# The modulation's matrix-vector products, moved from branches and projections into the attentions

## The chip, the cores and the metric

The kernel runs on one core of a Trainium2 chip. The metric is the device time of one execution in microseconds (us); given is the median of three runs. The engines are TensorE (PE, with its weight loads PEld), VectorE (DVE), ScalarE (ACT), GpSimd (POOL) and SyncE (SP), which here issues the DMAs. Each engine works through its own queue in order.

## The reference, cut to what matters

A first block of two layers with 512 tokens `x` and 256 tokens of context `ctx`, 2048 wide, then a second block. Everything is float32.

```python
for l in range(DEPTH):                                   # two layers
    sh_l, sc_l, g_l = split(silu(c)     @ w_mod[l] + b_mod[l], 3)
    sh_c, sc_c, g_c = split(silu(c_ctx) @ w_mod[l] + b_mod[l], 3)
    hl = xl * (1 + sc_l) + sh_l;  hc = xc * (1 + sc_c) + sh_c
    parts_l = split(hl @ w_in[l]);  parts_c = ...        # conv, attention, pooling
    att = differential attention of 8 heads over context and tokens
    out = concat(conv branch, attention, pooling branch) @ w_out[l]
    xl = layernorm(alpha * xl + g_l * out_l)             # the same for the context in layer 0
return second_block(xl, c)                               # modulated by one more product, w_ada
```

The modulations are products of a vector of 2048 with a matrix of 2048 x 6144: 48 columns of 128 values for each vector and layer. For `c` and `c_ctx` in layer 0 they are called `l0` and `c0`, in layer 1 `l1` and `c1`, and for the second block `s`. Columns 0 to 31 give shift and scale, 32 to 47 the gate. In layer 1 the gate of the context isn't needed.

## The kernel before

**Products on PE.** A float32 product is made of three matmuls: each 512 columns of weights are loaded (L158), rounded to the part `whi` on ACT (L159), and the rest `wlo` is subtracted on POOL or DVE (L139). A *unit* is 128 output columns for all tokens: 16 steps over the depth by three matmuls, for tokens (512 columns) and context (256), so 48 pairs at L166. Its sums stand in two of four `ps_m` buffers.

**Stages.** The first 322 us make layer 0's scale and shift and begin its first units. Then come: layer 0's attention (322 to 1070 us), its convolution and pooling tiles (`branch`, to 1336), the output projection of tokens (`w_out_group`, to about 1497) and context (to 1645), layer 1's attention (to 2345), its branches (to 2548), its projection, the second block. `conv_tile` makes a unit and copies it to `uu` on ACT (L514), makes a second one and multiplies it with `uu` on DVE into `V` (L521), then makes a third (L528).

**Dots.** Columns of the modulation that are not needed at once are made by `dots` (L776 to L812). It goes over four quarters of the depth. At a quarter's start it loads the conditioning vectors (`gv`, L787) and activates them (ACT L789, DVE L790). Then each step loads one 128 x 512 piece of weights into `gw` (L798) and makes one dot for each vector: on DVE in one instruction (L806), or, for every `pool_every`-th dot, as a product on POOL (L802) and a sum on ACT (L803). All these write one scratch buffer, tag `gj`. `gw` has `bufs` buffers, 2 in the attentions and 4 elsewhere.

**What sets the order.** `along(steps, n)` names the steps that go along with the units, `n` per unit; `advance` emits them with a priority lowered by 800, `finish` emits what is left. A scheduler then sets the order of each engine by priority and by when operands and buffers come free in its own model of time; on the chip the order is fixed. The widest products in layer 1's branches go another way (`gemv`): 1 MB of weights, 2048 wide, one DVE instruction each (L292), 30 of them.

Of the kernel before, what the change touches and what calls it, by code (L numbers as in the profile page):

```python
# [18 lines left out]
DRAM = bass.MemoryType.DRAM  # L19
# [26 lines left out]
def mixer_stack_kernel(ctx: ExitStack, tc: tile.TileContext, a: dict, out: bass.AP):  # L46
# [10 lines left out]

# [1 line left out]
    def ps_m(w=512):  # L59
# [10 lines left out]

# [1 line left out]
    ident = const.tile([128, 128], F32, name="ident")  # L72
# [54 lines left out]

# [1 line left out]
    Yd = [dp.tile([128, NT], F32, name=f"yd{k}") for k in range(KT)]  # L129
# [6 lines left out]

# [1 line left out]
    def sub_lo(lo, src, hi, eng):  # L138
# [9 lines left out]
    def load_chunk(*srcs, narrow=None):  # L148
        """512 columns at a time: the load, the part that float32r keeps and the exact rest"""
        n = 1 if narrow else 2  # L150
        hi, lo = (
            narrow.tile([128, 512], F32R, name=f"n{x}", tag=f"n{x}", bufs=2) if narrow else
            wp.tile([128, 1024], F32R, name=f"w{x}", tag=f"w{x}", bufs=3) for x in ("hi", "lo")
        )
        for i in range(n):
            sl = slice(i * 512, (i + 1) * 512)
            raw = wp.tile([128, 512], F32, name="wraw", tag="wraw", bufs=4)
            nc.sync.dma_start(raw, srcs[i] if len(srcs) == n else srcs[0][:, sl])  # L158
            nc.scalar.copy(hi[:, sl], raw)  # L159
            sub_lo(lo[:, sl], raw, hi[:, sl], lo_engine())  # L160
        return hi, lo
# [6 lines left out]
    def operands(*parts, c0=0):  # L168
        """parts: (psum columns, tiles by k) of a product's moving side"""
        return lambda k: [(ps, tuple(t[k][:, i, c0:c0 + ps.shape[-1]] for i in (0, 1))) for ps, t in parts]  # L170

    side = {"steps": iter(()), "n": 0, "late": 800}  # work of other engines that goes along with the units

# [35 lines left out]
    def side_units(n, zero=None):  # L209
        """psum of column tiles that are summed side by side, up to five with the zeros that let two of  # L210
        the narrow sums share a bank"""
        us = [Unit() for _ in range(n)]
        cs = ps_s()
        if zero is None:
            narrow = (cs[:, 0, :NCX], cs[:, 1, :NCX], ps_t()[:, :NCX], ps_v()[:, :NCX])
        else:
            narrow = [cs[:, i // 2, (i % 2) * NCX:(i % 2 + 1) * NCX] for i in range(4)] + [ps_v()[:, :NCX]]
            for b in range(2):
                nc.tensor.matmul(cs[:, b], zero[:, :128], zero, start=True, stop=False)
        for i, u in enumerate(us):  # L220
            u.lat = ps_m() if i < 4 else ps_t()
            u.cx = narrow[i]
            u.shared = zero is not None and i < 4
        us[0].close = cs if zero is not None else None
        return us
# [22 lines left out]
    def silu2(dst, src, tmp):  # L248
        """dst = 2 * silu(src)"""
        nc.scalar.activation(tmp, src, AF.Tanh, scale=0.5)  # L250
        nc.vector.scalar_tensor_tensor(dst, tmp, 1.0, src, op0=ALU.add, op1=ALU.mult)

# [1 line left out]
    mods = {}  # L254
# [8 lines left out]
    def silu_cvec(xp, c):  # L263
        """2 * silu of a conditioning vector that lies on all partitions"""
        t = xp.tile([128, 2, 512], F32, name="cth", tag="gjunk", bufs=1)
        for h in range(4):
            sl = slice(h * 512, (h + 1) * 512)
            nc.scalar.activation(t[:, h % 2], c[:, sl], AF.Tanh, scale=0.5)
            nc.vector.scalar_tensor_tensor(c[:, sl], t[:, h % 2], 1.0, c[:, sl], op0=ALU.add, op1=ALU.mult)

    def cvecs(xp, *idx):
        cs = [load_cvec(xp, i, f"ca{n}") for n, i in enumerate(idx)]
        for c in cs:
            silu_cvec(xp, c)
        return cs

# [8 lines left out]
    def dot(xp, wm, ca, dst, scale=0.5, last=False, split=False):  # L285
        """dst = scale * wm . ca; the last use of wm may overwrite it"""
        if last and split:
# [6 lines left out]
    def gemv(xp, src, vecs, wm_bufs=2, split=False):  # L294
        """vecs: (row vector on all partitions, modulation, bias, column)"""
        wm = load_gemv(xp, src, wm_bufs)
# [5 lines left out]
    def mod_row(name, c0, dst):  # L302
        """16 columns of a modulation tile as one row in DRAM"""
        tp = ps_t()
# [5 lines left out]
    def fold(name, g, b):  # L310
        """from 1+scale and shift to the scale and shift of the normalized rows"""
        m = mods[name]
# [7 lines left out]

# [1 line left out]
    def rope(tp, dst, ps):  # L322
# [174 lines left out]

# [1 line left out]
    def early_gate(xp, g):  # L499
        """a gate of layer 0 that was multiplied before the shifts were known"""  # L500
        t = xp.tile([128, NT], F32, name="pgr", tag="pgr", bufs=1)
# [86 lines left out]

# [1 line left out]
    def y_tiles(pool_, name, n, tag, ks=KT):  # L590
# [10 lines left out]
    def w_out_group(rp, w, Y, toks, res, gate, alpha, bufs=4, raw=False):  # L601
        """toks: (token tile of Y, row id); res(row, cc) -> residual chunk; returns normalized rows"""
        n = len(toks)
# [43 lines left out]
    def make_h(rp, rs, H, G, B, c0=0):  # L647
        """transposes the normalized rows, scales them and splits them into H"""
        n = len(rs)
# [43 lines left out]

    # =======================================================================
    # first block, layer 0
    # =======================================================================
    L, R = "left", "right"
# [11 lines left out]
    with pool("start", R) as sp:  # L709
# [10 lines left out]

        # the products with the scaled rows start before the shifts are known: the pool gates
        # get theirs later, as a bias
        zf = sp.tile([128, 512], F32, name="zf")
# [52 lines left out]
    def dots(xp, vecs, scale, srcs, dst, bufs, pool_every=0):  # L776
        """dst[v][:, i] = scale * srcs[i] . vecs[v], 512 columns at a time; a generator of the steps"""
        n = len(srcs)
# [47 lines left out]
    with pool("attn0", R) as ap_:  # L826
        along(itertools.chain(
            dots(ap_, ("sh_l", "sh_c"), 1.0, [a["w_gateT"][g] for g in range(8)], [pgb[:, 0], pgb[:, 1]], 2, 1),
            mod_dots1(ap_, 0, 32, 48, 2, 1),
        ), 3)  # L830
        attention(ap_, ap_, 0, w0, H, Hc, started=us)
# [27 lines left out]
    with pool("dots1", R) as gp:  # L859
        along(mod_dots1(gp, 1, 0, 20, 4), 10)  # L860
        branch(xp, xp, 0, H, Hc, NT, steps[1:])
        finish()
# [6 lines left out]
    new_mod("s")  # L869
    along(mod_dots1(rp, 1, 20, 32, 4), 2)  # L870
    rs = w_out_group(rp, a["w_out"][0], Y, [(t, t) for t in range(4)], res_dram(rp, a["x"]), "l0", ALPHA_1)
# [10 lines left out]
    Yc = [load_y(rp, t, NL, NCX, k) for k, t in zip(KORDER, y_tiles(cp, "yc0_", NCX, "c"))]  # L882
    along(mod_dots2(rp, 0, 2, 4), 1)
    rs = w_out_group(rp, a["w_out"][0], Yc, [(0, 0), (1, 1)], res_dram(rp, a["ctx"]), "c0", ALPHA_1)
# [7 lines left out]

    # =======================================================================
    # first block, layer 1
    # =======================================================================
    lo_plan["cycle"] = "P"
    with pool("attn1", L) as ap_:
        along(mod_dots2(ap_, 2, 34, 2, 1), 4)
        attention(ap_, aq, 1, a["w_in"][1], H, Hc)
        finish()  # L900
    es_q.close()
    xp = es_h.enter_context(pool("conv1", R))
    branch(xp, xa, 1, H, None, NL, steps[:1])
    with pool("gemv1", L) as gp:
        cl, cs = cvecs(gp, 0, 2)
        todo = [(a["w_mod"][1][n], [(cl, "l1", "b_mod1", n)]) for n in range(32, 48)]
        todo += [(a["w_ada"][0][n], [(cs, "s", "b_ada", n)]) for n in range(34, 48)]
        for i in range(4):
            for src, vecs in todo[8 * i:8 * i + 8]:
                gemv(gp, src, vecs)  # L910
            branch(xp, xa, 1, H, None, NL, steps[i + 1:i + 2])
        mod_row("l1", 32, "l1")
        mod_row("s", 32, "s")
        F_s = fold("s", P("ln_g1"), P("ln_b1"))
    es_y = ExitStack()
# [30 lines left out]

    # =======================================================================
    # second block
    # =======================================================================
    def proj(n):  # L950
# [251 lines left out]
def _layout(v):  # L1202
    """inputs of the program: the arrays of the reference, laid out; and constants of the shapes"""
    f = np.float32
# [91 lines left out]
```

## Time and profile before

| what | us |
|---|---|
| median of 3 runs | 3651.74 (3650.06 to 3652.78) |
| span of the profiled execution | 3643.0 |
| PE busy in it | 3384.8 |
| DVE busy | 2550.5 |
| POOL busy | 2063.3 |
| ACT busy | 1541.6 |
| dots on DVE (L806), 264 | 262.9 |
| dots' products on POOL (L802), 320 | 437.7 |
| their sums on ACT (L803), 320 | 201.9 |

The median lies 8.7 us above the span. Busy times of engines overlap; a wait of PE is what lengthens the span, since PE is busy nearly throughout.

### The profile page before, as it was taken

How to read it: one execution, taken by the hardware profiler on the slowest of the kernel's cores; microseconds unless marked ns; L12 is line 12 of the kernel's file. 1: busy time of each engine (PE TensorE's matmuls, PEld its weight loads, DVE VectorE, ACT ScalarE, POOL GpSimd, SP SyncE). 2: the span in 40 equal slices, each digit the busy share in tenths (PEclk: the TensorE clock that was granted, in tenths of full speed). 3: DMA queues.
4: the chain of work that ended last, by engine and by line, in shares of the span. 5: the costliest groups of instructions: out<-in, count | busy, mean ns of one | idle time of the engine just before them, and what ended most of it. 6: DMA issues, size and time to landing. Idle time of an engine off the chain costs nothing.

```text
span 3643.0 us, 47811 instructions
## 1 busy us (share of the span) xinstructions
PE 3384.8 (93%) x16462; PEld 2740.1 (75%) x16462; DVE 2550.5 (70%) x3817; ACT 1541.6 (42%) x3206; POOL 2063.3 (57%) x1420
## 2 busy tenths in 40 slices
PE   5779999999998788999999999999999899999997
PEld 4668778888887676778777777777778677777765
DVE  9994666666648888775566564485577798985666
ACT  4433666666531122244565553322445323244343
POOL 6665676666624543257777753478776344434432
PEclk8889999999999899999999999999999999999998
DMA  7542333323236556663444422486765222222565
GB/s 258 205 167 80 100 97 95 94 92 97 77 114 194 161 189 222 186 228 125 133 135 132 149 96 68 148 308 239 239 227 195 76 87 81 81 79 99 179 224 186
DMA packets 269140, 541.03 MB, mean 149 GB/s; under 512 B 30080, under 2 KB 37088, under 8 KB 260704
## 3 DMA queue, kind: packets, MB, share of 16 engines
q1 hardware_dynamic: 268896, 537.97, 44.7%
q8 instruction: 129, 2.11, 0.2%
q14 instruction: 115, 0.94, 0.1%
HBM read 508.05 MB, written 29.80 MB: 148 GB/s over the span
## 4 chain that ended last, share of the span: by engine, by line
PE 53%; DVE 24%; DMA 10%; issue 7%; POOL 3%; ACT 2%; SPq 0%; DVEq 0%; POOLq 0%; ACTq 0%
PE ps_m L166 39%; DVE acc L985 5%; DMA wraw<-in_w_out_dram 5%; DVE gpr L806 4%; PE ps_s L395 3%; DVE gjunk L292 2%; PE ps_s L392 2%; PE ps_v L433 2%; DVE wlo L139 2%; DVE h L139 1%; POOL wlo L139 1%; PE ps_t L423 1%; ACT whi L159 1%; DVE hf L766 1%; DVE wm L292 1%
## 5 line engine op out<-in xcount | busy, mean ns | idle before, releaser
L139 POOL TENSOR_TENSOR wlo<-wraw,whi 128x512 fp32r<-128x512 f32 x760 | 1121.4, 1492 | 914.4 <-ACT whi L159 808.4
L166 PE MATMUL ps_m<-h,whi 128*128 128x512 f32 (+1 forms) x4608 | 1577.7, 399 | 2.6 <-DVE qr L325 1.1
L166 PEld LDWEIGHTS ps_m<-h,whi 128*128 128x128 f32 x4608 | 867.9, 191 | 196.7 <-issue 9.9
L159 ACT CAST whi<-wraw 128x512 fp32r<-128x512 f32 x1032 | 602.9, 618 | 838.4 <-DMA wraw<-in_w_out_dram 264.8
L166 PE MATMUL ps_m<-h,wlo 128*128 128x512 f32 (+1 forms) x2304 | 914.9, 398 | 0.0
L802 POOL TENSOR_TENSOR gpr<-gw,gv 128x512 f32<-128x512 f32 x320 | 437.7, 1368 | 261.8 <-ACT gpr L803 207.6
L166 PE MATMUL ps_m<-hc,whi 128*128 128x256 f32 x1920 | 537.3, 286 | 0.0
L166 PEld LDWEIGHTS ps_m<-h,wlo 128*128 128x128 f32 x2304 | 439.4, 191 | 96.2 <-issue 2.7
L139 DVE TENSOR_TENSOR wlo<-wraw,whi 128x512 fp32r<-128x512 f32 x272 | 246.5, 917 | 180.1 <-ACT whi L159 178.7
L166 PEld LDWEIGHTS ps_m<-hc,whi 128*128 128x128 f32 x1920 | 363.1, 191 | 9.7 <-issue 5.8
L803 ACT ACTIVATE gpr<-gpr 128x512 f32<-128x512 f32 x320 | 201.9, 631 | 205.3 <-POOL gpr L802 202.6
L166 PE MATMUL ps_m<-hc,wlo 128*128 128x256 f32 x960 | 275.7, 287 | 0.0
L806 DVE SCALAR_TENSOR_TENSOR gpr<-gw,gv 128x512 f32<-128x512 f32 x264 | 262.9, 996 | 8.2 <-DMA gw<-in_w_ada_dram 1.7
L985 DVE SCALAR_TENSOR_TENSOR acc<-gu,pack,acc 128x511 f32<-128x511 f32 (+24 forms) x240 | 235.4, 993 | 5.4
L624 PE MATMUL ps_m<-wlo,y 128*128 128x512 f32 x512 | 206.9, 405 | 17.6 <-POOL wlo L139 11.1
L401 DVE TENSOR_REDUCE mx<-ps_s 128x1 f32<-128x768 f32 (+1 forms) x160 | 135.0, 844 | 113.4 <-PE ps_s L395 112.8
L625 PE MATMUL ps_m<-whi,y 128*128 128x512 f32 x512 | 202.9, 397 | 2.4 <-DVE y L139 1.6
L166 PEld LDWEIGHTS ps_m<-hc,wlo 128*128 128x128 f32 x960 | 183.7, 191 | 6.2 <-issue 4.3
L406 ACT ACTIVATE E<-ps_s,nb 128x768 f32<-128x768 f32 (+1 forms) x160 | 130.5, 816 | 133.4 <-DVE nb L403 130.4
L623 PE MATMUL ps_m<-whi,y 128*128 128x512 f32 x512 | 182.2, 398 | 0.4 <-ACT whi L159 0.2
L428 DVE TENSOR_TENSOR aTl<-ps_t,aTh 128x384 fp32r<-128x384 f32 (+1 forms) x144 | 77.2, 536 | 145.7 <-ACT aTh L427 145.4
L240 PE MATMUL ps_m<-h,whi 128*128 128x512 f32 x320 | 125.0, 438 | 58.1 <-DVE h L139 29.4
(372 smaller groups left out, 5778.6 us busy)
## 6 DMA issues: line engine op xcount, KB each, us to landing
wraw<-in_w_in_dram SPq DMA_DIRECT2D x640, 256.0 KB, 2.9
wraw<-in_w_out_dram SPq DMA_DIRECT2D x384, 256.0 KB, 3.5
wm<-in_w_mod_dram SPq DMA_DIRECT2D x48, 1024.0 KB, 5.7
gw<-in_w_mod_dram SPq DMA_DIRECT2D x192, 256.0 KB, 3.4
gw<-in_w_ada_dram SPq DMA_DIRECT2D x136, 256.0 KB, 3.1
wm<-in_w_ada_dram SPq DMA_DIRECT2D x14, 1024.0 KB, 5.5
yraw<-yd SPq DMA_DIRECT2D x40, 256.0 KB, 3.4
gw<-in_w_gateT_dram SPq DMA_DIRECT2D x32, 256.0 KB, 3.0
```

The lines of the kernel that those rows point to most:

```text
L139: eng.tensor_tensor(lo, src, hi.bitcast(F32), op=ALU.subtract)
L159: nc.scalar.copy(hi[:, sl], raw)
L166: nc.tensor.matmul(ps, w, mv[part], start=(first and p == 0), stop=(last and p == 2))
L401: nc.vector.reduce_max(mx, sv, axis=AX.XY)
L406: nc.scalar.activation(e[:, :nk].rearrange("p (c n) -> p c n", c=nch), sv, AF.Exp, bias=nb, scale=0.125, accum_out=d,)
L623: nc.tensor.matmul(ps, yh, hi[:, sl], start=(k == 0), stop=False)
L624: nc.tensor.matmul(ps, yh, lo[:, sl], start=False, stop=False)
L625: nc.tensor.matmul(ps, yl, hi[:, sl], start=False, stop=(k == KT - 1))
L802: nc.gpsimd.tensor_tensor(pr, w, t, op=ALU.mult)
L803: nc.scalar.activation(pr, pr, AF.Copy, scale=scale, accum_out=part[v][:, i:i + 1])
L806: nc.vector.scalar_tensor_tensor(junk, w, scale, t, op0=ALU.mult, op1=ALU.mult, accum_out=part[v][:, i:i + 1])
L985: nc.vector.scalar_tensor_tensor(A[:, s:], U[:, :NL - s], wj(i), A[:, s:], op0=ALU.mult, op1=ALU.add)
```

## The change

It moves dots between stages, in the arguments of `along`, and removes the `gemv` loop of layer 1's branches with `cvecs`. Comments go too, so that lines from about 275 on have numbers six lower in the changed file (L806 becomes L800, L802 L796, L803 L797, L798 L792, L514 L508, L521 L515).

```diff
@@ layer 0, attention
             mod_dots1(ap_, 0, 32, 48, 2, 1),
-        ), 3)
+            mod_dots1(ap_, 1, 0, 32, 2, 3),
+        ), 8)
         attention(ap_, ap_, 0, w0, H, Hc, started=us)
@@ layer 0, branches
-        along(mod_dots1(gp, 1, 0, 20, 4), 10)
+        along(mod_dots(gp, ("l1",), (0,), a["w_mod"][1], "b_mod1", 32, 48, 4), 4)
         branch(xp, xp, 0, H, Hc, NT, steps[1:])
@@ layer 0, projection of the tokens, then of the context
-    along(mod_dots1(rp, 1, 20, 32, 4), 2)
+    along(mod_dots2(rp, 0, 4, 4), 1)
...
-    along(mod_dots2(rp, 0, 2, 4), 1)
+    along(mod_dots2(rp, 4, 8, 4), 1)
@@ layer 1, attention
-        along(mod_dots2(ap_, 2, 34, 2, 1), 4)
+        along(itertools.chain(mod_dots2(ap_, 8, 28, 2, 2), mod_dots2(ap_, 28, 48, 2, 2)), 5)
         attention(ap_, aq, 1, a["w_in"][1], H, Hc)
@@ layer 1, branches
-    with pool("gemv1", L) as gp:
-        cl, cs = cvecs(gp, 0, 2)
-        todo = [(a["w_mod"][1][n], [(cl, "l1", "b_mod1", n)]) for n in range(32, 48)]
-        todo += [(a["w_ada"][0][n], [(cs, "s", "b_ada", n)]) for n in range(34, 48)]
-        for i in range(4):
-            for src, vecs in todo[8 * i:8 * i + 8]:
-                gemv(gp, src, vecs)
-            branch(xp, xa, 1, H, None, NL, steps[i + 1:i + 2])
-        mod_row("l1", 32, "l1")
+    branch(xp, xa, 1, H, None, NL, steps[1:5])
+    mod_row("l1", 32, "l1")
```

The dots by stage, before and after:

| stage | on POOL and ACT | on DVE | loads of `gw` |
|---|---|---|---|
| layer 0, attention | 192, then 280 | 0, then 168 | 96, then 224 |
| layer 0, branches | 0 | 160, then 64 | 80, then 64 |
| layer 0, projection, tokens | 0 | 96, then 16 | 48, then 16 |
| layer 0, projection, context | 0 | 8, then 16 | 8, then 16 |
| layer 1, attention | 128, then 80 | 0, then 80 | 128, then 160 |
| layer 1, branches | 0 | 30 wide, then 0 | 30 of 1 MB, then 0 |

The order of the engines at the end of layer 0's attention. First ACT, before: the copies of the first convolution unit to `uu` stand right behind attention's last operations (`rt`, `o2`).

```order
L439 ACTIVATE o2_9349<-ps_v_9341 128x256
L442 CAST o2h_9351<-o2_9349 128x256
L159 CAST whi_10088<-wraw_10090 128x512
L159 CAST whi_10088<-wraw_10094 128x512
L453 COPY rt_9149<-ps_v_9355 128x256
L455 ACTIVATE rt_9149<-rt_9149,eps_t_78 128x256
L514 COPY uu_9951<-ps_m_9833 128x512
L514 COPY uu_9951<-ps_m_9834 128x256
```

ACT, changed: behind the same `rt` stand the sums of the remaining layer-1 dots, some 70 rows of L797, and then the copies.

```order
L447 COPY rt_10152<-ps_v_10358 128x256
L449 ACTIVATE rt_10152<-rt_10152,eps_t_78 128x256
...
L797 ACTIVATE gpr_10005,gpart_9413<-gpr_10005 128x512
L797 ACTIVATE gpr_10016,gpart_9413<-gpr_10016 128x512
L797 ACTIVATE gpr_10025,gpart_9413<-gpr_10025 128x512
L508 COPY uu_10858<-ps_m_10740 128x512
L508 COPY uu_10858<-ps_m_10741 128x256
```

The copies moved behind the sums. On DVE, before: attention's last operation (`SG`), then the branch.

```order
L460 RECIPROCAL rt_9149<-rt_9149 128x256
L461 TENSOR_TENSOR SG_9025<-SG_9025,rt_9149 128x256
L519 MEMSET V_9954 128x1
L520 MEMSET V_9954 128x1
L519 MEMSET V_9954 128x1
L520 MEMSET V_9954 128x1
L504 TENSOR_SCALAR pgr_10206<-pgr_10206,pgb_167 128x512
```

On DVE, changed: 133 dots between the two, the last of them of the fourth quarter (`gpart` holds a quarter's partial sums).

```order
L455 TENSOR_TENSOR SG_10028<-SG_10028,rt_10152 128x256
L800 SCALAR_TENSOR_TENSOR gpr_6745,mod_c1_166<-gw_6741,gv1_6162 128x512
L800 SCALAR_TENSOR_TENSOR gpr_6752,mod_c1_166<-gw_6747,gv1_6162 128x512
...
L800 SCALAR_TENSOR_TENSOR gpr_10023,gpart_9413<-gw_10021,gv0_9403 128x512
L806 TENSOR_TENSOR mod_l1_165<-mod_l1_165,gpart_9413 128x32
...
L513 MEMSET V_10861 128x1
L514 MEMSET V_10861 128x1
```

The branch's first operations moved behind them. POOL's 68 products and the loads of these dots stand in one piece too, with no remainder of weights (`wlo`) and no other load between them. PE's own queue, changed, where the third unit (`ps_m_10993`) follows the second (`ps_m_10863`):

```order
L166 MATMUL ps_m_10862<-h0_15_146,wlo_10923 128x512
L166 MATMUL ps_m_10863<-hc0_15_162,wlo_10923 128x256
L299 MATMUL ps_t_11126<-ident_69,mod_l0_163 16x128
L166 MATMUL ps_m_10993<-h0_0_131,whi_10995 128x512 x2
L166 MATMUL ps_m_10993<-h0_0_131,wlo_10996 128x512
```

The units follow each other on PE as before; nothing moved in between.

## Rows read from the trace of the kernel before

**Rows 1.** The page, busy time, share of the span and instructions of each engine.
```profile
PE 3384.8 (93%) x16462; PEld 2740.1 (75%) x16462; DVE 2550.5 (70%) x3817; ACT 1541.6 (42%) x3206; POOL 2063.3 (57%) x1420
```

**Rows 2.** Stretches: length, busy PE, PEld, DVE, ACT, POOL (instructions), PE clock, DMA, GB/s.
```profile
322.00:1070.00 748.00, 740.22 (x4083) 607.88 (x4082) 459.67 (x756) 439.18 (x1015) 480.27 (x356) 0.99 0.29 91
1083.00:1336.00 253.00, 208.68 (x1090) 178.82 (x1089) 223.03 (x441) 45.18 (x83) 118.44 (x78) 0.90 0.56 176
1336.00:1497.00 161.00, 151.11 (x621) 119.71 (x620) 137.80 (x284) 45.18 (x86) 51.95 (x38) 0.96 0.70 220
...
1645.00:2345.00 700.00, 698.55 (x3527) 557.72 (x3527) 381.44 (x592) 359.26 (x788) 444.52 (x335) 1.00 0.36 115
2345.00:2548.00 203.00, 192.59 (x798) 152.62 (x797) 141.89 (x147) 54.60 (x97) 159.38 (x93) 0.97 0.79 281
```

**Rows 3.** PE's waits, 1083 to 1336: line waited for, us, times, longest.
```profile
PE ps_v L166 <- ACT dh L569: 26.5, 4, 10.7
PE ps_v L166 <- DVE yp L584: 13.1, 4, 5.5
```

**Rows 4.** Timeline of ACT at attention's end: start, us, operation, idle before.
```profile
1070.12 0.84 ACT L514 COPY uu<-ps_m 128x512 f32<-128x512 f32 x2
```

**Rows 5.** Timeline of DVE there.
```profile
1072.04 0.43 DVE L461 TENSOR_TENSOR SG<-SG,rt 128x256 f32<-128x256 f32 x1
...
1084.52 1.01 DVE L521 TENSOR_TENSOR V<-ps_m,uu 128x512 f32<-128x512 f32 x2
```

**Rows 6.** Timeline of PE there.
```profile
1083.32 0.39 PE L166 MATMUL ps_m<-h,whi 128*128 128x512 f32 x1
```

**Rows 7.** Line L802 in layer 0's attention: count, ns min/median/max, first and last start.
```profile
L802 POOL TENSOR_TENSOR gpr<-gw,gv x192: 1271/1292/2039, 346.2 to 981.0; 128x512 f32<-128x512 f32 x192
```

**Rows 8.** Timeline of POOL in head 7.
```profile
949.55 1.30 POOL L802 TENSOR_TENSOR gpr<-gw,gv 128x512 f32<-128x512 f32 x1 [0.83 <-ACT gpr L803]
951.68 1.29 POOL L802 TENSOR_TENSOR gpr<-gw,gv 128x512 f32<-128x512 f32 x1 [0.83 <-ACT gpr L803]
```

**Rows 9.** Line L803 in layer 0's attention.
```profile
L803 ACT ACTIVATE gpr<-gpr x192: 613/632/661, 347.5 to 982.3; 128x512 f32<-128x512 f32 x192
L803 ACT ACTIVATION_READ_ACCUMULATOR gpr<-gpr x192: 183/187/218, 348.1 to 982.9; 128x1 f32 x192
```

**Rows 10.** Timeline of DVE in the layer-0 branches, then of POOL.
```profile
1103.28 1.66 DVE L806 SCALAR_TENSOR_TENSOR gpr<-gw,gv 128x512 f32<-128x512 f32 x1
...
1115.02 0.69 DVE L806 SCALAR_TENSOR_TENSOR gpr<-gw,gv 128x512 f32<-128x512 f32 x1
...
1115.76 0.69 DVE L806 SCALAR_TENSOR_TENSOR gpr<-gw,gv 128x512 f32<-128x512 f32 x1
...
1099.25 5.14 POOL L139 TENSOR_TENSOR wlo<-wraw,whi 128x512 fp32r<-128x512 f32 x3
1117.03 1.11 POOL L565 TENSOR_TENSOR dd<-S,rc 128x512 f32<-128x512 f32 x1 [12.64 <-DMA yd<-yc]
```

**Rows 11.** DMA issues, median us to landing: layer 0's attention, then its branches.
```profile
gw<-in_w_mod_dram SPq DMA_DIRECT2D x64, 256.0 KB, 3.0
...
gw<-in_w_mod_dram SPq DMA_DIRECT2D x79, 256.0 KB, 3.7
```

**Rows 12.** Timeline of all engines where a quarter ends and the next begins.
```profile
766.79 0.19 ACT L803 ACTIVATION_READ_ACCUMULATOR gpr<-gpr 128x1 f32 x1
...
770.81 1.50 POOL L802 TENSOR_TENSOR gpr<-gw,gv 128x512 f32<-128x512 f32 x1 [4.75 <-ACT E L406]
```

**Rows 13.** Stretches of the layer-0 branches, columns as in rows 2.
```profile
1099.85:1335.10 235.25, 190.93 (x988) 163.21 (x987) 206.54 (x414) 39.18 (x73) 108.54 (x71) 0.89 0.55 171
...
1250.00:1260.00 10.00, 3.01 (x9) 2.63 (x10) 8.91 (x13) 1.86 (x3) 9.39 (x8) 0.56 0.41 128
```

**Rows 14.** Groups of DVE, 2345 to 2548: busy us, mean ns, idle before, releasers.
```profile
L292 DVE SCALAR_TENSOR_TENSOR wm<-wm,ca 128x2048 f32<-128x2048 f32 x30 | 78.5, 2615 | 24.5 <-DMA wm<-in_w_ada_dram 13.9 <-DMA wm<-in_w_mod_dram 10.5
```

**Rows 15.** PE's waits in layer 0's projections, 1336 to 1645.
```profile
PE ps_s L624 <- DVE wlo L139: 9.7, 4, 4.7
```

More of the change, by code (lines that the diff above doesn't have):

```diff
@@ L269, in silu_cvec @@
             nc.vector.scalar_tensor_tensor(c[:, sl], t[:, h % 2], 1.0, c[:, sl], op0=ALU.add, op1=ALU.mult)
[L271 to L275, printed above, removed]
     def new_mod(name):
@@ L903, in mixer_stack_kernel @@
     branch(xp, xa, 1, H, None, NL, steps[:1])
-    with pool("gemv1", L) as gp:
-        cl, cs = cvecs(gp, 0, 2)
-        todo = [(a["w_mod"][1][n], [(cl, "l1", "b_mod1", n)]) for n in range(32, 48)]
-        todo += [(a["w_ada"][0][n], [(cs, "s", "b_ada", n)]) for n in range(34, 48)]
-        for i in range(4):
-            for src, vecs in todo[8 * i:8 * i + 8]:
-                gemv(gp, src, vecs)
-            branch(xp, xa, 1, H, None, NL, steps[i + 1:i + 2])
-        mod_row("l1", 32, "l1")
-        mod_row("s", 32, "s")
-        F_s = fold("s", P("ln_g1"), P("ln_b1"))
+    branch(xp, xa, 1, H, None, NL, steps[1:5])
+    mod_row("l1", 32, "l1")
+    mod_row("s", 32, "s")
+    F_s = fold("s", P("ln_g1"), P("ln_b1"))
     es_y = ExitStack()
```

## The prediction, written before the result was known

> **What bounds the kernel now.** The summary of the page comes first: TensorE (PE) is busy 93% of a span of 3643.0 us, VectorE (DVE) 70% [rows 1]. So a gain must come out of the 7% in which PE idles, and a loss comes from whatever makes PE idle more. Next, the stretches [rows 2]. In layer 0's attention PE is busy 740 of 748 us, in layer 1's 698.6 of 700, and there DVE, ScalarE (ACT) and GpSimd (POOL) all have room: 440 to 480 us of 748. In the layer-0 branches (1083 to 1336) PE is busy 209 of 253 us while DVE is busy 223 and the granted clock is 0.90. In the projection behind it and in the layer-1 branches PE misses 10 us each. Third, whom PE waits for in the branches [rows 3]: 40 us in eight waits, on ACT and DVE in the pooling tiles, work that queues behind the dots on DVE. So dots do cost time in the branches, and the attentions have idle engines. That is the case for the change. Last I ask, engine by engine, where the moved dots stand in the new program, since every engine works its queue in order.
>
> **Where they stand.** Layer 0's own dots run on POOL and ACT. They are 192 pairs, from 346.2 to 981.0 us, and attention's last DVE operation starts at 1072.04 [rows 5, 7]. The change asks for eight steps per unit instead of three, but the order of all engines is the same up to the last head: these 192 pairs keep their slots. Layer 1's dots for both vectors (4 quarters of 32 steps, a step being one load and two dots) therefore start only at about 985 us. Most of the first quarter is mixed with head 7; its last five steps and the other three quarters stand behind attention's last operation, in one piece, on DVE, POOL, ACT and the DMA queue alike: 68 POOL dots with their ACT halves and 133 DVE dots. I call it the tail.
>
> **What waits for it.** In the kernel before ACT copies the first convolution unit out of PSUM at 1070.12, right behind attention [rows 4]. PE, which finished the second unit, starts the third at 1083.3 [rows 6], in the two buffers that this copy freed (there are four, two per unit). In the changed kernel the same copy stands behind the last ACT half of the tail, and DVE's first branch operations stand behind its last dot. PE's queue holds nothing else between the second and third unit. So PE stops near 1083 until the tail is done; the tail has no cover.
>
> **Length of the tail.** All dots write one scratch buffer, so they form one chain over the engines.
> - A POOL-ACT dot takes 2.13 us from start to start (949.55 to 951.68: 1.30 on POOL, 0.63 and 0.19 on ACT) [rows 8, 9].
> - A DVE dot takes 0.74 us with POOL quiet (1115.02 to 1115.76) and 1.66 with POOL at work [rows 10]. In the tail the one buffer keeps the two from overlapping, so 0.74 holds.
> - Every third dot goes to POOL, so three steps of two dots cost 2.87, 2.87 and 1.48 us, 2.41 on average.
> - A step's weights come into one of two buffers, and a load can be issued only when the step two before it is done. A load lands in 3.0 us here, 3.7 where DMA is busier [rows 11]; with the handing over I take 3.15. A step ends at the later of (the step before) and (the step two before, plus 3.15), plus its dots. Followed through 32 steps that gives 94.7 us behind the first load, or 2.96 a step: two buffers don't hide the loads.
> - At a quarter's start the conditioning vectors are reloaded and activated: 3.8 us from the last half dot (766.98) to the next dot (770.81) [rows 12]. I take 5, since other work helps less here. A quarter is 100 us.
>
> The end is 1072 + 5 (head 7 delayed by 42 DVE dots of its own) + 5 x 3 + 3 x 100 = 1392 us, so PE starts the third unit at 1393 instead of 1083: **+310**. Bounds: with all loads hidden a quarter is 78 + 4 = 82, the end 1333 and the term +250. With 3.7 for a load and 7.5 at a boundary it is 103.9 - 3.7 + 7.5, say 108, plus 10 more for head 7, and the term is +345.
>
> The Trainium skill, page "DMA: Bandwidth & Descriptors", section "Anatomy of one DMA", fits a load (on POOL's path; here SyncE issues) as 2.0 us plus bytes over 436 GB/s. For 256 KB that is 2.6 us, under the 3.0 of the row. By it the three quarters would be about 17 us shorter; the row decides.
>
> **The other terms.**
> - Clock: in the 10 us in which PE worked 3.0 the granted clock was 0.56 [rows 13], near the lower of the two levels (1.2 of 2.4 GHz). After the stall some matmuls run at half speed: **+4** (0 to +8).
> - Layer-0 branches: DVE loses 96 of 160 dots there, some 100 us at a mean near 1.05. From the end of the third unit 235 us are left for ten units [rows 13]; a unit is 48 pairs of matmuls at 0.348 us, 167 us in all, so 68 are lost. The pooling chains' latency stays, the queue in front of them goes: **-28** (-45 to +5, the latter if loads for 48 fewer steps make no odds and the new order is worse).
> - Projection of layer 0: 96 dots become 16; PE waits there 9.7 us on DVE's remainder of the weights [rows 15] and a few more on others; the context's projection gets 8 dots more: **-10** (-18 to 0).
> - Layer-1 branches: the 30 wide products go (78.5 us of DVE) with 30 loads of 1 MB [rows 14], for 10 us of PE idle: **-10** (-16 to 0).
> - Layer-1 attention: 128 POOL dots become 80, and 80 DVE dots come. Their last stands well ahead of attention's last operation in every queue, so no tail. DVE goes from 381 to at most 381 + 80 x 1.74 = 520 of 700 us: **+3** (0 to +10).
>
> Sum: 310 + 4 - 28 - 10 - 10 + 3 = **+269**. The span becomes 3912; the median lies 8.7 above the profiled span, so 3921 us.
>
> **Rivals.**
> 1. *The tail is shorter* because loads land faster or overlap better with an idle DMA. Its price is +250 for the stall, so 3651.7 + 250 - 41 = 3861. For it: nothing but these loads is queued there. Against: 3.0 is already the median of 64 such loads beside attention [rows 11].
> 2. *The tail is longer*: loads at 3.7, boundaries at 7.5, head 7 late. +345 - 41 gives 3956; if the branches gain nothing either, 3997. For it: 3.7 and more was seen in the branches. Against: DMA was busy 0.56 there [rows 2] and carries one stream here.
> 3. *It pays, as meant*: PE isn't held. It needs the copy of the first unit ahead of the tail, or PE work for 300 us that needs no eviction. Then only the gains stay, -28 - 10 - 10 + 8 = -40, so about 3612. It decides from where the tail's end falls before 1083, which even 68 x 2.13 + 133 x 0.74 = 243 us of bare dots exclude. Only a misread order leaves room.
> 4. *DVE and POOL slow each other in the attentions.* A dot on DVE went from 0.69 to 1.66 us beside POOL [rows 10]. If each of the 42 + 80 DVE dots there cost PE half of that 1 us, it is +60, so about 3980. Against: PE waited for hardly anything in 748 and 700 us. The Trainium skill, "GPSIMD Engine Reference", section "Specifications", says that POOL shares its SBUF interfaces with VectorE and contends with DVE instructions of two SBUF inputs; the dots are such, and the trace agrees.
>
> **How the numbers follow.** Forecast 0.78, rival 1 0.07, rival 2 0.08, rival 4 0.03, rival 3 0.03, no change (gains and losses cancel) 0.01. From the terms' ends the forecast spans about 3870 to 3965. I widen it to 3845 to 4000 for rivals 1, 2 and 4. Within 0.2%, about what a measurement can tell: 0.01; faster 0.03; slower 0.96.
>
> **What would show it.** Right: a stretch from about 1085 to 1390 with PE at zero, DVE with runs of dots some 0.74 or 2.9 us apart, PE's longest wait there naming ACT's copy of the first unit, and a low clock behind it; branches behind it with less wait on the pooling chain; no waits in layer 1's attention. Wrong: PE busy in that stretch, or the first unit's copy near 1075. If the stall is there but its length is off, the loads' landing and the period of three steps (8.9 us with loads, 7.2 without) tell which term failed.

## The result, and the profile after

The changed kernel takes 3926.7 us (3922.3 to 3930.3) against 3652.3 us for the kernel before on the same chip: the ratio is 1.075, with a 95% interval of 1.0736 to 1.0763. The forecast was 3921 us. The profiled span is 3920.5 us instead of 3643.0, so 277.5 us have to be found.

They can be placed by the times at which PE begins a part of its work, since its order is the same up to layer 1: the third unit of the branches (1083.3 before), the token projection (1335.2), the context's (1540.3), its end (1646.9), layer 1's projection (2549.3).

| part | before, us | after, us | difference | forecast |
|---|---|---|---|---|
| to the third unit | 1083.3 | 1376.8 | +293.5 | +310 |
| rest of layer 0's branches, clock in it | 251.9 | 227.3 | -24.6 | +4 - 28 |
| layer 0's projections | 311.7 | 299.7 | -12.0 | -10 |
| layer 1's attention and branches | 902.4 | 924.0 | +21.6 | +3 - 10 |
| the rest | 1093.7 | 1092.7 | -1.0 | 0 |

The stretches of the changed kernel, columns as in [rows 2]:

```profile
1084.00:1376.00 292.00, 1.42 (x9) 0.98 (x7) 99.88 (x278) 56.26 (x148) 90.68 (x72) 0.51 0.34 100
1376.00:1386.00 10.00, 9.21 (x45) 7.95 (x46) 7.33 (x28) 3.82 (x10) 4.13 (x2) 0.82 0.61 180
1376.80:1604.10 227.30, 199.56 (x1081) 173.20 (x1082) 128.37 (x252) 43.64 (x82) 106.09 (x77) 0.92 0.57 178
1604.10:1796.90 192.80, 183.54 (x770) 146.19 (x769) 98.33 (x167) 52.13 (x98) 60.18 (x45) 0.98 0.56 185
1796.90:1903.80 106.90, 99.72 (x449) 79.11 (x448) 76.97 (x98) 46.45 (x79) 61.16 (x44) 0.97 0.66 221
1903.80:2640.00 736.20, 709.29 (x3517) 557.30 (x3516) 441.87 (x760) 328.06 (x694) 383.18 (x285) 1.00 0.39 122
2640.00:2827.80 187.80, 187.39 (x805) 150.15 (x804) 31.63 (x49) 49.96 (x90) 115.07 (x93) 1.00 0.40 129
```

The first of them is the stall: 292 us with 9 matmuls, DVE busy a third of it, POOL not even that, DMA at 0.34, and the granted clock 0.51, near the lower of its two levels (1.2 of 2.4 GHz). The last two are layer 1's attention and its branches. Before, they were:

```profile
1646.90:2345.00 698.10, 696.65 (x3519) 556.17 (x3518) 381.15 (x592) 358.22 (x787) 442.75 (x334) 1.00 0.36 115
2345.00:2549.30 204.30, 193.89 (x803) 153.68 (x802) 141.89 (x147) 54.60 (x97) 159.38 (x93) 0.97 0.79 281
```

For the same matmuls (3519 and 3517) attention takes 38 us longer. PE's idle time makes 25 of them, 26.9 us instead of 1.5; the other 13 are counted as busy, for which no run shows a cause. The branches take 16.5 us less and have no idle left, where before they had 10 us of it.

PE's waits from 1050 to 1700 (line waited for, us, times, longest) put the stall at one single wait, and the pooling waits that answer to [rows 3] fell from 40 to 28 us:

```profile
PE ps_m L166 <- ACT uu L508: 291.4, 1, 291.4
PE ps_v L166 <- ACT dh L563: 20.7, 2, 12.5
PE ps_v L166 <- DVE yp L578: 7.1, 2, 5.2
```

Attention's last DVE operation in the timeline, and then the end of the stall (to be held against [rows 4], [rows 5] and [rows 6]):

```profile
1082.43 0.41 DVE L455 TENSOR_TENSOR SG<-SG,rt 128x256 f32<-128x256 f32 x1
```

```profile
1376.18 0.84 ACT L508 COPY uu<-ps_m 128x512 f32<-128x512 f32 x2
...
1376.79 1.22 PE L166 MATMUL ps_m<-h,whi 128*128 128x512 f32 x2 [291.37 <-ACT uu L508]
...
1376.90 1.00 DVE L515 TENSOR_TENSOR V<-ps_m,uu 128x512 f32<-128x512 f32 x2
```

The copy of the first unit (L508, which was L514) starts at 1376.18 instead of 1070.12, PE right behind it, with 291.37 us of idle ahead of it. Attention itself ended at 1082.4, ten us later than before.

Inside the tail, the timeline over three steps, POOL's products and one of ACT's halves:

```profile
1121.55 1.26 POOL L796 TENSOR_TENSOR gpr<-gw,gv 128x512 f32<-128x512 f32 x1 [3.12 <-DMA gw<-in_w_mod_dram]
...
1125.16 1.26 POOL L796 TENSOR_TENSOR gpr<-gw,gv 128x512 f32<-128x512 f32 x1 [2.35 <-DVE gpr L800]
...
1126.99 0.19 ACT L797 ACTIVATION_READ_ACCUMULATOR gpr<-gpr 128x1 f32 x1
...
1129.60 1.26 POOL L796 TENSOR_TENSOR gpr<-gw,gv 128x512 f32<-128x512 f32 x1 [3.18 <-DMA gw<-in_w_mod_dram]
```

And the timeline from the last sum of a quarter to the first product of the next:

```profile
1191.51 0.19 ACT L797 ACTIVATION_READ_ACCUMULATOR gpr<-gpr 128x1 f32 x1
...
1197.27 1.26 POOL L796 TENSOR_TENSOR gpr<-gw,gv 128x512 f32<-128x512 f32 x1 [6.32 <-DMA gw<-in_w_mod_dram]
```

Three steps take 8.05 us (1121.55 to 1129.60). The products wait in turn for a load and for DVE's dot. A quarter's start costs 5.6 us (1191.70 to 1197.27).

### The profile page after: what moved, and what is told of

Same layout as the page of the kernel before. It is cut to its first block, busy times and chain, and to the rows that moved or that the text cites. A ratio compares the mean times of both kernels' runs of the same rounds, so it can differ in the third digit from the quotient of the medians.

```text
span 3920.5 us, 48420 instructions
## 1 busy us (share of the span) xinstructions
PE 3370.0 (86%) x16462; PEld 2725.0 (70%) x16462; DVE 2468.3 (63%) x3887; ACT 1567.5 (40%) x3282; POOL 2063.4 (53%) x1460
## 5 line engine op out<-in xcount | busy, mean ns | idle before, releaser
L166 PE MATMUL ps_m<-h,whi 128*128 128x512 f32 (+1 forms) x4608 | 1572.1, 398 | 295.2 <-ACT uu L508 291.4
L139 POOL TENSOR_TENSOR wlo<-wraw,whi 128x512 fp32r<-128x512 f32 x760 | 1099.2, 1463 | 913.4 <-ACT whi L159 820.1
L796 POOL TENSOR_TENSOR gpr<-gw,gv 128x512 f32<-128x512 f32 x360 | 478.1, 1328 | 552.8 <-DMA gw<-in_w_mod_dram 153.8
L800 DVE SCALAR_TENSOR_TENSOR gpr<-gw,gv 128x512 f32<-128x512 f32 x344 | 291.5, 847 | 331.5 <-ACT gpr L797 148.5
L797 ACT ACTIVATE gpr<-gpr 128x512 f32<-128x512 f32 x360 | 227.2, 631 | 511.2 <-POOL gpr L796 509.2
L618 PEld LDWEIGHTS ps_m<-wlo,y 128*128 128x128 f32 x512 | 96.8, 189 | 51.2 <-POOL wlo L139 20.8
```

The costliest lines, as they stand in the source:

```text
L139: eng.tensor_tensor(lo, src, hi.bitcast(F32), op=ALU.subtract)
L166: nc.tensor.matmul(ps, w, mv[part], start=(first and p == 0), stop=(last and p == 2))
L618: nc.tensor.matmul(ps, yh, lo[:, sl], start=False, stop=False)
L796: nc.gpsimd.tensor_tensor(pr, w, t, op=ALU.mult)
L797: nc.scalar.activation(pr, pr, AF.Copy, scale=scale, accum_out=part[v][:, i:i + 1])
L800: nc.vector.scalar_tensor_tensor(junk, w, scale, t, op0=ALU.mult, op1=ALU.mult, accum_out=part[v][:, i:i + 1])
```

## The experiments

### The layer-1 half by itself: e1, e2, e3

The part that the forecast had wrong comes first: layer 1's attention got 38 us slower, not 3. In the changed kernel PE's waits there (1903 to 2828) are short and many, all on attention's own operations on ACT and DVE, and DVE's own waits (1904 to 2640) show what stands in front of those operations. First PE's:

```profile
PE ps_s L386 <- ACT E L400: 9.3, 12, 1.9
PE ps_t L417 <- DVE E L411: 4.0, 5, 1.5
PE ps_v L427 <- ACT aTh L421: 2.4, 4, 1.3
```

Then DVE's:

```profile
DVE gpr L800 <- DMA gw<-in_w_ada_dram: 52.6, 24, 4.1
...
DVE gpr L800 <- ACT gpr L797: 33.0, 16, 3.7
```

DVE waits 53 us for the loads of its dots and 33 for the ACT half of the dot ahead. Three kernels part these, all made from the kernel before, with layer 0 as it was.

**e1**: the layer-1 part alone, as near as it goes. Columns 2 to 47 of `s` are dots in layer 1's attention (the changed kernel has 8 to 47 there), and the 16 wide products of `l1` stay in the branches.

```diff
-        along(mod_dots2(ap_, 2, 34, 2, 1), 4)
+        along(itertools.chain(mod_dots2(ap_, 2, 28, 2, 2), mod_dots2(ap_, 28, 48, 2, 2)), 5)
...
-        cl, cs = cvecs(gp, 0, 2)
+        cl, = cvecs(gp, 0)
         todo = [(a["w_mod"][1][n], [(cl, "l1", "b_mod1", n)]) for n in range(32, 48)]
-        todo += [(a["w_ada"][0][n], [(cs, "s", "b_ada", n)]) for n in range(34, 48)]
```

> The kernel before with the layer-1 part of the change alone: the modulation s from column 2 on as dots in layer 1's attention, every second one on POOL and ACT, the others on DVE (184 steps instead of 128), and only the 16 gate columns of layer 1 left as wide products in the branches. In the changed kernel layer 1's attention lost some 27 us of PE and its branches won some 11. Theory (DVE dots hold up attention, whatever else was changed): attention loses 25 to 31, the branches win about 5, so 3670 to 3680 us. Rival (the loss in the changed kernel is a late effect of layer 0's stall, such as other prefetching): 3645 to 3652 us.

Measured: 3685.6 us, ratio 1.0077 (1.0056 to 1.0097). The part alone makes the kernel slower, by 6 us more than the end of my range: layer 1's attention and branches take 941.1 us instead of 902.4. The rival falls.

**e2**: the same 184 dots, all on POOL and ACT (against e1).

```diff
-mod_dots2(ap_, 2, 28, 2, 2), mod_dots2(ap_, 28, 48, 2, 2)
+mod_dots2(ap_, 2, 28, 2, 1), mod_dots2(ap_, 28, 48, 2, 1)
```

> As e1, but all 184 dots of layer 1's attention on POOL and ACT as before the change, none on DVE. Theory (a DVE dot at the head of DVE's queue is what holds up attention): PE's waits on attention's own DVE and ACT results go, attention costs what it cost before (700 us, 1 to 3 us of waits), the branches keep their gain of about 5: 3645 to 3652 us, 20 to 30 below e1. Rival (more dots of any kind in attention cost time): 3665 us and more.

Measured: 3636.4 us, ratio 0.994 (0.9925 to 0.9955): faster than both kernels, and 9 us under my range. Attention and branches take 891.6 us, 11 less than before; that is twice the gain that I gave the branches. The profiled spans differ by 10 us (3632.9 and 3643.0, on two chips), the medians on one chip by 20.

**e3**: e1 with one load per quarter for all its steps.

```diff
-                w = xp.tile([128, 512], F32, name="gw", tag="gw", bufs=bufs)
-                nc.sync.dma_start(w, src[:, sl])
+                if i == 0 or pool_every != 2:
+                    w = xp.tile([128, 512], F32, name="gw", tag="gw", bufs=bufs)
+                    nc.sync.dma_start(w, src[:, sl])
```

> As e1, but the dots of layer 1's attention load their weights once per quarter and pass, and all its steps read that piece (so s is not the reference's): the dots, their engines and their order of work stay, the waits on loads go. Theory A (DVE's queue stands while a dot at its head waits for a load): most of the 25 to 31 us goes, 3650 to 3658 us. Theory B (DVE and POOL slow each other when both read): nothing goes, 3670 to 3680 us. Theory C (DVE dots wait for the ACT half of the dot ahead, which has the one scratch buffer): a third goes at most.

Measured: 3647.2 us, ratio 0.9965 (0.9947 to 0.9983). Attention and branches take 901.2 us, 40 less than in e1. That is theory A, and more of it than expected: the net loss goes whole. The stretches from the end of layer 0's projections to PE's last matmul of attention (L447), columns as in [rows 2], of the kernel before, e1, e2 and e3:

```profile
1646.90:2333.80 686.90, 685.45 (x3471) 547.13 (x3470) 373.75 (x585) 350.68 (x776) 436.51 (x329) 1.00 0.36 115
1643.30:2374.70 731.40, 703.40 (x3470) 553.35 (x3469) 443.10 (x777) 329.68 (x708) 398.08 (x293) 0.99 0.42 130
1649.70:2335.00 685.30, 683.14 (x3461) 546.11 (x3460) 395.93 (x587) 385.67 (x885) 511.81 (x382) 1.00 0.45 138
1646.30:2330.30 684.00, 679.46 (x3436) 542.39 (x3436) 438.49 (x777) 330.59 (x704) 395.31 (x291) 1.00 0.22 70
```

Attention loses 44 us in e1. In e2 and e3 it takes as long as before; 10 and 35 of its 3471 matmuls have moved behind that point, some 2 and 8 us by the mean of 0.2 us each, an estimate. So e2 has the whole loss back, and e3 all but a few us of it.

The waits between 1640 and 2360, first of e1: those of DVE for its dots, and PE's longest, for attention's exponentials.

```profile
DVE gpr L806 <- DMA gw<-in_w_ada_dram: 61.7, 29, 5.4
DVE gpr L806 <- ACT gpr L803: 56.2, 29, 4.9
```

```profile
PE ps_s L392 <- ACT E L406: 13.8, 15, 3.1
```

The same of e3:

```profile
DVE gpr L807 <- ACT gpr L804: 49.2, 38, 2.2
```

```profile
PE ps_s L392 <- ACT E L406: 2.3, 2, 2.1
```

In e3 DVE still waits 49 us for ACT's halves, and its dots still run beside POOL (one takes 875 ns on average, 942 in e1); PE waits 4.5 us in all, where it waited 1.3 before. So the one scratch buffer and the sharing of DVE and POOL cost attention a few us at most, and theories B and C fall as the cause of the loss. What costs is that DVE's queue stands while the dot at its head waits for a load, with attention's operations behind it. That it isn't the traffic of the loads shows in e2, which loads as much. There POOL waits for them, and PE hardly for anything (PE's waits in layer 1's attention, then POOL's):

```profile
PE ps_m L166 <- DVE qr L325: 1.1, 1, 1.1
```

```profile
POOL gpr L802 <- ACT gpr L803: 88.4, 79, 3.2
...
POOL gpr L802 <- DMA gw<-in_w_ada_dram: 23.6, 15, 2.6
```

### Where the stall comes from: e4, e9, e10

The forecast took from the order of the queues that everything of the branches stands behind the tail, without saying why. By the code, the buffers of attention and of its dots come from one pool, which closes when all of them are done; what the branches need is allocated after that. **e4** takes the buffers of all dots of layer 0's attention from a pool of their own that stays open through the branches:

```diff
+    dp0 = es_h.enter_context(pool("dots0", L))
     with pool("attn0", R) as ap_:
...
-            mod_dots1(ap_, 1, 0, 32, 2, 3),
+            mod_dots1(dp0, 1, 0, 32, 2, 3),
         ), 8)
         attention(ap_, ap_, 0, w0, H, Hc, started=us)
-        finish()
...
-        along(mod_dots(gp, ("l1",), (0,), a["w_mod"][1], "b_mod1", 32, 48, 4), 4)
+        side["steps"] = itertools.chain(side["steps"], mod_dots(gp, ("l1",), (0,), a["w_mod"][1], "b_mod1", 32, 48, 2))
```

> The changed kernel, but the dots of layer 0's attention take their buffers from a pool of their own that stays open through the branches, and attention doesn't finish them first; the 16 gate columns follow in the branches with two buffers. Theory (the tail stands in one piece because the pool of attention's buffers closes only when the dots are done, and all that is allocated after it waits): ACT's copy of the first unit comes near 1080, PE starts the third unit near 1085, and the dots spread over the branches. By the period of 2.7 us a step the 128 steps end near 1350 and the 64 of the gate near 1500, so a shorter stall of 100 to 170 us stands at the branches' end: 3750 to 3820 us. Rival (there are simply too many dots for DVE and POOL, wherever they stand): PE loses the same 290 us, spread, about 3925 us.

Measured: 3910.8 us, ratio 1.069 (1.0672 to 1.0709). The first half of the theory holds; the second misses by far, and the time is nearly the rival's, though in two waits and not spread. The copy's first start moved to 1078.4, PE ran through the branches and reached the projection near 1310. Then it stood, twice (the copies, with their first and last start; PE's waits from 1000 to 1700; and a stretch with columns as in [rows 2]):

```profile
L508 ACT COPY uu<-ps_m x8: 368/468/578, 1078.4 to 1276.7; 128x512 f32<-128x512 f32 x4, 128x256 f32<-128x256 f32 x4
```

```profile
PE ps_t L299 <- DVE grow L301: 154.2, 1, 154.2
PE ps_m L617 <- ACT y L591: 111.3, 1, 111.3
```

```profile
1340.00:1480.00 140.00, 0.00 (x0) 0.00 (x0) 50.19 (x139) 28.52 (x78) 46.54 (x39) 0.50 0.36 109
```

The first wait is for a copy (`grow`, L301) that, by the code, shares its buffer with the partial sums of the dots, the second for tiles of the projection that are allocated after the branches' pools. Beside the branches the dots are slow: their second quarter took 168 us (1094 to 1263), the third 119, the last, alone, 90. So they end at 1481, the gate's 64 at 1592. My expectation had counted 2.7 us a step throughout and had not seen the shared buffer; the miss is both. The stall moved from the place where attention's pool closes to that buffer, and then to the place where the branches' pools close.

Since e4 changes several things, **e9** and **e10** repeat it with fewer dots, on the kernel of e7 (below), and with a buffer of its own for `grow`. e10 has 12 columns for 8.

```diff
-            mod_dots1(ap_, 1, 0, 8, 2, 1),
+            mod_dots1(dp0, 1, 0, 8, 2, 1),
         ), 3)
         attention(ap_, ap_, 0, w0, H, Hc, started=us)
-        finish()
...
-        along(mod_dots1(gp, 1, 8, 20, 4), 10)
+        along(itertools.chain(side["steps"], mod_dots1(gp, 1, 8, 20, 3)), 10)
```

To make room the branches get one early tile of the projection less (`early_y`, 5 for 6), and the dots in the branches three load buffers for four.

> As e7 (columns 0 to 7 of l1 and c1 as 64 dots on POOL and ACT behind layer 0's own), but the dots' buffers lie in a pool that stays open through the branches, the row copied for the gates has a buffer of its own, and the remaining 96 DVE dots of the branches get three load buffers instead of four. Theory (e7's 80 us stall is the closing of the pool, not the dots): the first unit's copy comes near 1072, no stall at the third unit, the 64 dots run on beside the branches and end well before them; the branches keep e7's gain: 3618 to 3632 us. Rival (the dots cost PE their time wherever they stand, as the 3911 us of e4 suggest): 3670 to 3705 us.

Measured: 3642.3 us, ratio 0.9958 (0.9944 to 0.9973), 59 us under e7. The 80 us stall of e7 is gone, with the same dots on the same engines. It is 10 above the range I gave; PE now waits 16 us for tiles of the projection. One thing e9 doesn't part: it leaves out attention's `finish` together with the closing, and `finish` emits what is left of the dots ahead of the branches. By the code it does so at a lowered priority, which speaks for the closing as the cause, but no run has the one without the other.

> As e9 with columns 0 to 11: 96 dots on POOL and ACT, 64 left to DVE in the branches. The POOL dots take 96 x 2.13 us and more beside the weights' remainders, from about 985 to 1230 or 1260, still inside the branches, which end at 1335. Theory of e9: no stall, DVE a little freer, 3612 to 3630 us. Rival: 3700 us and more.

Measured: 3683.4 us, ratio 1.0067 (1.0049 to 1.0085), between the theory's time and the rival's. No stall at the third unit either; PE reached the projection at 1294 instead of 1335 and then waited 92 us for those tiles. The last product's sum starts at 1345 in that kernel, later than the 1260 that I expected. PE's waits from 1060 to 1700, of e9:

```profile
PE ps_v L166 <- DVE yp L584: 19.8, 3, 11.5
PE ps_v L166 <- ACT dh L569: 19.4, 4, 9.9
PE ps_m L623 <- ACT y L597: 15.6, 3, 9.9
```

And of e10:

```profile
PE ps_m L623 <- ACT y L597: 92.7, 2, 92.0
```

### How long the stall is: e5, e6, e7

**e5** is the changed kernel whose layer-1 dots in layer 0's attention load only once per quarter, by the edit of e3 with `pool_every != 3`.

> The changed kernel, but layer 1's dots in layer 0's attention load their weights once per quarter and all 32 steps read that piece (so l1 and c1 are not the reference's). Theory (the tail's period of 2.68 us a step is set by loads into two buffers on top of the chain of dots): the chain alone is 7.2 us per three steps, 2.4 a step, so a quarter goes from 92 to about 83 us and PE's stall from 291 to 258 to 268 us; one run near 3898 us. Rival 1 (loads were hidden, the chain alone sets it): no change, 291 us. Rival 2 (loads set it alone): the stall falls under 230 us.

Measured: one run, 3907.3 us. The stall is 266 us instead of 291, and three steps take 7.26 us instead of 8.05 (PE's wait from 1060 to 1700, then POOL's timeline):

```profile
PE ps_m L166 <- ACT uu L508: 266.0, 1, 266.0
```

```profile
1239.93 1.26 POOL L797 TENSOR_TENSOR gpr<-gw,gv 128x512 f32<-128x512 f32 x1 [2.37 <-DVE gpr L801]
1243.56 1.26 POOL L797 TENSOR_TENSOR gpr<-gw,gv 128x512 f32<-128x512 f32 x1 [2.37 <-DVE gpr L801]
1247.19 1.26 POOL L797 TENSOR_TENSOR gpr<-gw,gv 128x512 f32<-128x512 f32 x1 [2.37 <-DVE gpr L801]
```

So the chain of dots makes nine tenths of the tail and the loads the rest, as the theory had it. The time is 9 us above the expected one, but not in what the edit touches: PE reaches layer 1's projection at 2803.7 instead of 2827.8, and what follows took 1101.8 us in this one execution instead of 1092.7.

**e6** and **e7** are the kernel of e2 with columns 0 to 3, or 0 to 7, of `l1` and `c1` moved into layer 0's attention, where they are made by POOL and ACT.

```diff
             mod_dots1(ap_, 0, 32, 48, 2, 1),
+            mod_dots1(ap_, 1, 0, 4, 2, 1),
...
-        along(mod_dots1(gp, 1, 0, 20, 4), 10)
+        along(mod_dots1(gp, 1, 4, 20, 4), 10)
```

> The kernel of e2 with columns 0 to 3 of l1 and c1 moved from the layer-0 branches into layer 0's attention, all on POOL and ACT: 32 dots behind the 192. Theory (what ends before attention's last unit costs nothing, only what stands behind it is a stall): 32 x 2.13 us and four quarter starts of 5.6 from about 985 end near 1080, before PE needs the copy; no stall, and the branches lose 32 of 160 DVE dots for a gain of 3 to 9: 3627 to 3634 us. Rival (any layer-1 dots there delay the copy by their whole length): a stall of some 90 us, 3715 us.

> As e6 with columns 0 to 7: 64 dots. By the same account they take 64 x 2.13 + 4 x 5.6 = 159 us and some delay by head 7, so they end at 1145 to 1170, 60 to 85 us after PE has stopped at 1083; the branches lose 64 of 160 DVE dots for a gain of 8 to 18: 3680 to 3712 us. If the stall is a matter of the number of dots alone and not of where they end, it is 64/256 of 291 us, 73 us, which is the same here, and half of it, 36, in e6.

Measured: e6 3636.1 us, ratio 0.9942 (0.9927 to 0.9957), the time of e2 and 2 us over the range; e7 3700.9 us, ratio 1.0124 (1.0109 to 1.0139), inside. PE's wait for the copy in e6:

```profile
PE ps_m L166 <- ACT uu L514: 6.5, 1, 6.5
```

And in e7:

```profile
PE ps_m L166 <- ACT uu L514: 79.9, 1, 79.9
```

A stall of 6.5 us for 32 dots and of 80 for 64 is no share of the whole: what ends before PE needs the copy is free, and each us beyond that point is a us of stall. The copy starts at 1093.3 in e6 and at 1165.0 in e7, 72 us apart; the stalls are 73 apart. e6 was to end at 1080 and ended at 1093; its branches won back what the stall cost and 5.5 us more (the projection begins at 1329.5, in e2 at 1335.0), but its median is e2's.

### What holds up the branches: e8

**e8** is the kernel of e2 with every third of the branches' dots on POOL and ACT, and three scratch buffers in that place.

```diff
-        along(mod_dots1(gp, 1, 0, 20, 4), 10)
+        along(mod_dots1(gp, 1, 0, 20, 4, 3, 3), 10)
...
-                        pr = xp.tile([128, 512], F32, name="gpr", tag="gj", bufs=1)
+                        pr = xp.tile([128, 512], F32, name="gpr", tag="gj", bufs=gjb)
```

> The kernel of e2 with every third of the 160 dots of the layer-0 branches on POOL and ACT and three scratch buffers there: 54 dots leave DVE (about 57 us of its 222), POOL goes from 118 to about 190 of 252 us. Theory (DVE's load is what PE's waits in the branches go back to): the waits on the pooling tiles' ACT and DVE operations fall, 8 to 20 us: 3616 to 3628 us. Rival (the chain of the pooling tiles or POOL's part in it sets them): nothing or slower, 3634 to 3650 us.

Measured: 3642.8 us, ratio 0.9963 (0.9949 to 0.9978), 6 above e2, though the two intervals overlap. The waits on the pooling tiles stay (45 us, in e2 44), and a stretch from 1083 to 1335 has DVE at 207 instead of 223 us and POOL at 200 instead of 117:

```profile
PE ps_v L166 <- ACT dh L569: 32.3, 3, 14.0
PE ps_v L166 <- DVE yp L584: 13.2, 3, 7.0
```

```profile
1083.00:1335.00 252.00, 199.53 (x1058) 172.28 (x1057) 206.76 (x317) 78.63 (x189) 199.50 (x134) 0.89 0.55 171
```

The rival holds: POOL makes the weights' remainders and much of the pooling tiles, and with more work for it the waits on the same places stay. DVE was to shed 57 us and shed 16, because its remaining operations got slower, the dots among them (L806 in the branches: ns min/median/max; the kernel before, then e8):

```profile
L806 DVE SCALAR_TENSOR_TENSOR gpr<-gw,gv x160: 669/692/2317, 1090.0 to 1325.3; 128x512 f32<-128x512 f32 x160
L806 DVE SCALAR_TENSOR_TENSOR gpr<-gw,gv x104: 676/1394/2343, 1088.7 to 1308.2; 128x512 f32<-128x512 f32 x104
```

With POOL at 200 of 252 us the median of a dot on DVE went from 692 to 1394 ns. In the changed kernel the branches won 25 us, with 96 dots fewer and none on POOL.

## Why the prediction was right, point by point

**The place of the tail and the wait: right.** One wait of 291.4 us on ACT's copy, at the place named, with PE idle from 1085 to 1377 and the low clock. The cause behind the order, which the prediction didn't have, is by e7 and e9 the pool that closes (with its `finish`).

**The length: 293.5 instead of 310.** Head 7's delay was 10 us, not 5, and the step into a quarter 5.6, not 5. The period of three steps is the term that was mis-sized: 8.05 us, forecast 8.9. I had let a load be issued when the step two before it was *done*. The buffer is free when its last reader has read it; for a dot on POOL that is the end of POOL's product, and ACT's half (0.63 + 0.19 us [rows 9]), which comes once in three steps at the place that counts, is not in the load's way. The rows of the tail show it: the product of 1125.16 ends at 1126.42 and its ACT half at 1127.18; the product at 1129.60 waited for the load into that buffer and starts only 2.42 us after the half, while the fastest load in the stall took 2.9 us. 8.88 - 0.82 is 8.06. Three whole quarters took 92 us each instead of 100 (from 1101.6 to 1193.4, to 1285.1 and to 1376.3). e5 bears out the rest of the model: without loads 7.26, forecast 7.2. The 17 us that the forecast gave for loads of 2.6 us leave out the handing over of 0.15 that its other sums have; with it they are 12, by the same steps.

**Branches and projections of layer 0: right in size**, -24.6 for -24 and -12.0 for -10.

**Layer 1's attention: wrong.** The term was +3 with 0 to +10, and the stretches say +38 (736.2 us instead of 698.1). The sign that went with it, no waits in layer 1's attention, failed too. The branches behind it won 16.5, forecast 10 with up to 16. I had bounded attention's term by DVE's busy time, 520 of 700 us, which asks only whether DVE has room. e1 to e3 show what is paid: the waits of the dot at the head of DVE's queue, 53 us in the changed kernel, with attention's work queued behind. Rival 4 named the right place with the wrong mechanism. A dot on DVE ran slower beside POOL, 1.66 us instead of 0.69 [rows 10], and in e3, where dots still run beside POOL, attention loses a few us at most. The Trainium skill ("GPSIMD Engine Reference", section "Specifications") has the two contend for their shared SBUF interfaces when DVE's instruction has two SBUF inputs; the trace agrees, and e8's 1394 ns do too.

The errors, -16.5 us at the stall and +28.6 in layer 1 (+35 in attention, -6.5 in the branches), made most of each other up. That the time came within 6 us of the forecast is in part luck.

**The rivals.** Rival 1 (loads that land faster or overlap better) holds in its second half: loads landed no faster, 3.0 us, but the shorter quarters took some 25 us of the 60 that it would have taken, and head 7's delay and the quarters' starts gave some back. Rival 3, that it pays, fails as the forecast said, since the dots don't fit in front of 1083; with the pool open (e4) most of the loss comes back at two other buffers. The two layers' parts pay differently: e2, which moves only `s` and keeps it on POOL, is 0.6% faster than the kernel before, and no move of layer 1's dots into layer 0's attention on top of it (e6, e7, e9, e10) came out clear of e2.

Open are the 13 us of longer busy time in layer 1's attention, the part of `finish` in e9, and what e9 would be with all early tiles of the projection; that wasn't tried.

## What to carry to other kernels

Before moving work into a stage with idle engines, ask when its chain ends there, and what closes with it: a pool of buffers that waits for the last of them is a barrier for all that is allocated after. Count a serial chain over engines by its period, not by the engines' busy time; the free capacity was there (DVE a third busy in the stall) and of no use. And give work that waits for loads to an engine behind which nothing urgent is queued: the same 184 dots made attention and branches 39 us longer on DVE and POOL in turn (e1), and 11 us shorter on POOL alone (e2).

## What the runs showed of the hardware

Dots on DVE whose operands were at hand hardly held up attention although POOL read beside them (e3: 875 ns a dot on average with a median of 693, PE's waits 4.5 us in some 700). A load of 256 KB landed in 3.0 us in the stall too, with nearly nothing else in the queues, as beside attention [rows 11]: an otherwise idle DMA made the single load no faster. With POOL busy 200 of 252 us the median dot on DVE took twice its time (e8, above). After 292 us at the lower clock PE's first 10 us had a granted clock of 0.82; the branches behind it, at 0.92, were not worse off than before, at 0.90.
